# Up projection: the first of four sums of weight blocks formed by two transfers of GpSimd's queue instead of by VectorE

## The chip, the cores and the metric

One core of a Trainium2 chip. The metric is the device time of one execution in microseconds (us), the median over several runs. TensorE is called PE here, VectorE DVE, ScalarE ACT, GpSimd POOL and SyncE SP, as the profile does.

## The reference

One encoder layer for two sequences of 512 and 256 tokens (768 in all), width 2048, float32: a Fourier group and windowed attention side by side, an output projection, then the MLP. The part that matters here is the MLP's first product:

```python
h = rmsnorm(x, ln_mlp_g)
u = jax.nn.relu(h @ w_up)        # w_up: 2048 x 8192
x = x + (u * u) @ w_down         # w_down: 8192 x 2048
```

## The kernel before

Every float32 product is made of three products of rounded parts: a factor is split into a high part (rounded by ACT, `wh`) and a low part (the rest, by DVE, `wl`), and PE multiplies high by high, high by low and low by high.

The up projection multiplies with Strassen's scheme in Winograd's form. K (2048) is cut in two halves `kh`, the 8192 columns into 16 groups `g` of 512; a unit is one half and one group, so there are 32 units, the first 16 with `kh` 0. A unit's piece of `w_up` is four blocks of 128 partitions x 4 x 256 numbers (512 KB): a11, a12 (left 256 columns, even and odd rows of K) and a21, a22 (right 256 columns). Seven products per unit need as left factors a11, a12, a22 and four sums: s1 = a21 + a22, s2 = s1 - a11, s3 = a11 - a21, s4 = a12 - s2. In the order of steps 0 to 6 the products use a11, a12, s2, s1, s3, s4, a22 (table `steps`); s3 and s4 overwrite a21 and a12. Step s of unit u is written (u,s) below, and each is 24 matmuls of 128 x 384.

`up_load` (L846) brings a block by SP's queue into tiles `ur` (tag `raw` with 2 buffers for a11 and a12, `ur` with 4 for a21 and a22). `up_sum` (L851) forms a sum on DVE; s1 and s2 go into tiles `sx` (2 buffers, so s1 of the next unit takes the place of s1 of this one). `up_high` (L868) rounds a factor on ACT, `up_low` (L874) takes the rest on DVE, `up_product` (L888) multiplies into PSUM `pu`, `up_out` moves a result from PSUM into a tile `o` (ACT copies, L906, or DVE adds, L909). `up_step` runs ahead: while PE does step q = 7u + s, DVE makes the low part of step q + 2, and the sum and the high part are those of step q + 3.

In the first 16 units `x2_load` (L983) brings quarters of x back on POOL's queue (tiles `xq`, in units 1, 4, 7, 10 after step 1), `x2_sums` (L988) and `x2_split` work on them, and POOL writes the parts back (L1001). In unit 15 POOL loads the right factors of the second half over those of the first, six transfers `xf` of 1.5 MB (L974), each as soon as PE has done the step that read the old one. In the second half it brings the first half's results back into tiles `o` (L899). `yp` (L798) are additions of POOL for the stage before.

Each engine works through its queue in order. The order on PE, ACT and DVE in this stage is that of the program's text; on POOL and SP a scheduler sets it. A transfer waits on its queue before it is issued, and what stands behind it waits too.

Of the kernel before, what the change touches and what calls it, by code (L numbers as in the profile page):

```python
# [11 lines left out]
F32 = mybir.dt.float32  # L12
# [3 lines left out]
ALU = mybir.AluOpType  # L16
# [4 lines left out]
P = 128  # L21
# [19 lines left out]
def hybrid_encoder(ctx: ExitStack, tc: tile.TileContext, a: dict):  # L41
    nc = tc.nc
    ctx.enter_context(tc.manual_schedule(engines={mybir.EngineType.PE}))

    def f32(ap):
        return ap.bitcast(F32)
# [60 lines left out]
    w_up = a["w_up"].rearrange("(k p) c -> p k c", p=P)  # L107
# [43 lines left out]
    with ExitStack() as ph:  # L151
# [260 lines left out]
        units = [(b, g) for b in range(NM) for g in range(NKV)]  # L412
# [241 lines left out]
    def at(t, fn):  # L654
        clock[1] += 1
        heapq.heappush(events, (t, clock[1], fn))
# [9 lines left out]
    for u in range(len(units)):  # L666
        t = pace * u
# [165 lines left out]
    units = [(kh, g) for kh in range(2) for g in range(NG)]  # L833
    pp = ctx.enter_context(tc.tile_pool(name="pp5", bufs=4, space=PSUM, reuse_waits="tile"))
    uw, uo, ux, ups = {}, {}, {}, {}
    C11, C12, C22, C21 = range(4)

    def up_load(u, name):
        if u >= len(units):
            return  # L840
        kh, g = units[u]
        c, par = int(name[1]) - 1, int(name[2]) - 1
        pool, tag, bufs = (wpool, "raw", 2) if c == 0 else (up, "ur", 4)
        raw = pool.tile([P, 4, 256], F32, tag=tag, name="ur", bufs=bufs)
        c0 = g * 512 + c * 256
        nc.sync.dma_start(raw[:], w_up[:, 8 * kh + par : 8 * kh + 8 : 2, c0 : c0 + 256])  # L846
        uw[u, name] = raw

    def up_sum(u, s):
        name = steps[s][0]  # L850
        op_ = lambda out, x, y, op: nc.vector.tensor_tensor(out=uw[u, out][:], in0=uw[u, x][:], in1=uw[u, y][:], op=op)  # L851
        if s == 1:
            uw[u, "s1"] = up.tile([P, 4, 256], F32, tag="sx", name="sx", bufs=2)
            op_("s1", "a21", "a22", ALU.add)
        elif s == 2:
            uw[u, "s2"] = up.tile([P, 4, 256], F32, tag="sx", name="sx", bufs=2)
            op_("s2", "s1", "a11", ALU.subtract)
        elif s == 4:
            uw[u, "s3"] = uw[u, "a21"]
            op_("s3", "a11", "a21", ALU.subtract)  # L860
        elif s == 5:
            uw[u, "s4"] = uw[u, "a12"]
            op_("s4", "a12", "s2", ALU.subtract)

    def up_high(u, s):
        raw = uw[u, steps[s][0]]
        wh = wpool.tile([P, 4, 256], F32R, tag="wh", name="wh", bufs=4)
        nc.scalar.activation(wh[:], raw[:], AF.Copy)  # L868
        ux[u, s] = (raw, wh)

    def up_low(u, s):
        raw, wh = ux[u, s]
        wl = wpool.tile([P, 4, 256], F32R, tag="wl", name="wl", bufs=4)
        nc.vector.tensor_tensor(out=wl[:], in0=raw[:], in1=f32(wh[:]), op=ALU.subtract)  # L874
        ux[u, s] = (wh, wl)

    def up_product(u, s):
        kh, g = units[u]
        _, f, bank = steps[s]
        if s == first_of[bank]:  # L880
            ups[u, bank] = pp.tile([P, 2, 512], F32, tag="ps", name="pu")
        ps = ups[u, bank]
        wh, wl = ux.pop((u, s))
        xb = right[kh][s]
        for t in range(2):
            for i in range(4):
                for n, (w, o) in enumerate(((wh, 0), (wh, 1), (wl, 0))):
                    nc.tensor.matmul(  # L888
                        ps[:, t, :HALF], w[:, i, t * P : (t + 1) * P], xb[:, o, i, :],
                        start=(s == first_of[bank] and i == 0 and n == 0), stop=(i == 3 and n == 2),  # L890
                        skip_group_check=(s != first_of[bank]),
                    )
# [3 lines left out]
    def up_tile(u, q, load=False):  # L896
        o = uo[u, q] = up.tile([P, 2, HALF], F32, tag="o", name="o", bufs=10)
        if load:
            nc.gpsimd.dma_start(o[:], p_d[q][units[u][1]][:])  # L899
        return o  # L900
# [25 lines left out]
    def up_out(u, s):  # L926

        if units[u][0] == 0:
            q, bank, how = ((C11, "X", "copy"), (C11, "Z", "add"), (C12, "X", "copy"), (C22, "Y", "copy"), (C22, "X", "add"), (C12, "Y", "add"), (C21, "X", "copy"))[s]
            up_take(u, q, bank, how)  # L930
            if s in (1, 4, 5, 6):
                up_put(u, q)
            return
        q, bank = ((C11, "X"), (C11, "Z"), (C12, "X"), (C22, "Y"), (C22, "X"), (C12, "Y"), (C21, "X"))[s]
        up_take(u, q, bank, "add")
        if s in (1, 4, 5, 6):
            up_relu2(u, q, {C11: s_d[2], C22: s_d[3], C12: a21_d}.get(q))

    def up_after(u, s):


        if u < 0 or units[u][0] == 0:
            return
        if s == 0:
            up_left(u, 0, C11, C22, ALU.add)
        elif s == 3:
            up_left(u, 5, C12, C11, ALU.subtract)
        elif s == 4:
            up_left(u, 6, C21, C22, ALU.subtract)
            up_left(u, 4, C11, C21, ALU.add)  # L950
            for q in range(4):
                del uo[u, q]

    def up_step(u, s):

        q = 7 * u + s
        at = lambda d: divmod(q + d, 7)
        more = lambda d: q + d < 7 * len(units)
        if more(2):
            up_low(*at(2))  # L960
        up_product(u, s)
        if more(3):
            up_sum(*at(3))
            up_high(*at(3))
        if q > 0:
            up_out(*at(-1))
        up_after(u - 1, s)
        for x in {0: ("a21", "a22"), 1: ("a11",), 3: ("a12",)}.get(s, ()):
            up_load(u + 1, x)
        if u + 1 < len(units) and units[u + 1][0] == 1 and s in (2, 3, 5, 6):  # L970
            up_tile(u + 1, {2: C11, 3: C12, 5: C22, 6: C21}[s], True)
        if u == NG - 1 and s < 6:

            nc.gpsimd.dma_start(f32(xf[:, steps[s][1]]), x2_d[steps[s + 1][1]][:])  # L974
            right[1].append(xf[:, steps[s][1]])
# [50 lines left out]
    up = up_ctx.enter_context(tc.tile_pool(name="up", bufs=1, reuse_waits="tile"))  # L1026
    for x in ("a21", "a22"):
        up_load(0, x)
    up_sum(0, 1)
    up_sum(0, 2)  # L1030
    up_high(0, 2)
    up_low(0, 2)
# [147 lines left out]
    for u in range(len(units)):  # L1180
        for s in range(2 if u == 0 else 0, 7):
            up_step(u, s)
            x2_jobs.get((u, s), lambda: None)()
            if u == 0 and s == 3:
                for x in pts:
                    x1_factors(*x)
                bctx.close()
            if u == 13 and s == 0:
                xs = up_ctx.enter_context(tc.tile_pool(name="xs", bufs=1, side="right", reuse_waits="tile")).tile([P, 2, 4, HALF], F32R, tag="xs", name="xs")
                nc.gpsimd.dma_start(f32(xs[:]), x2_d[steps[0][1]][:])  # L1190
                right.append([xs])
            if u == UL and s == 3:
                loads(0)
            if u == UL and s == 5:
                sums(0)
                lows(0)
            if u == UL and s == 6:
                up_after(UL, 0)
# [152 lines left out]
```

## Time and profile before

| | |
|---|---|
| median of 3 runs | 2660.26 us (2658.65 to 2661.46) |
| profiled execution: span | 2660.9 us (no other time of it is listed) |
| PE busy | 2606.8 us, 98% |
| DVE busy | 1732.0 us, 65% |
| ACT busy | 1060.1 us, 40% |
| POOL busy | 265.1 us, 10% |
| moved by DMA | 468.31 MB, mean 176 GB/s |

The span runs from the first to the last instruction of one profiled execution. Rows of the profile name a line of the kernel, an engine, an operation and its tiles, out<-in; waits name who waited, for whom, the total in us, how often, and the longest. A list of DMA issues gives KB each and the median us from issue to landing. A row of a timeline starts with the start and the duration in us, and in brackets has the idle time before it and what ended it.

### The profile page before, as it was taken

To read this page: it belongs to the slowest core of one execution; us is meant where nothing else is said; L and a number is where in the kernel's file an instruction comes from. 1 tells how busy PE (TensorE), PEld (TensorE's weight loads), DVE (VectorE), ACT (ScalarE), POOL (GpSimd) and SP (SyncE) were. 2 spreads that over 40 slices of the span, in tenths; PEclk is the share of its full clock that TensorE was granted. 3 is DMA by queue.
4 is the path that set the end of the run, shared out by engine and by line. 5 is a ranking of instruction groups with operands and counts; after the bars stand their busy time and mean duration, and the time that the engine had idled before them with its cause. 6 is when DMAs were issued, how large, how long until landed. Compare 5 with 4: busy or idle time off the path is not lost.

```text
span 2660.9 us, 35017 instructions
## 1 busy us (share of the span) xinstructions
PE 2606.8 (98%) x13652; PEld 2376.5 (89%) x13652; DVE 1732.0 (65%) x2100; ACT 1060.1 (40%) x1523; POOL 265.1 (10%) x375
## 2 busy tenths in 40 slices
PE   8999998998999999998999999999999999999998
PEld 8999997877889999998999999978888888888886
DVE  6334446766746565654777777747776775777677
ACT  5233326664433333332545444433333333333335
POOL 1011212334210010101000000020000000000000
PEclk9999999999999999999999999999999999999999
DMA  5323464444664454547666666585553672554364
GB/s 172 122 93 109 140 202 146 121 127 150 205 219 159 157 188 160 182 151 278 199 227 231 212 217 230 188 326 178 178 176 99 203 255 65 180 186 157 102 206 145
DMA packets 261094, 468.31 MB, mean 176 GB/s; under 512 B 26240, under 2 KB 157824, under 8 KB 259392
## 3 DMA queue, kind: packets, MB, share of 16 engines
q1 hardware_dynamic: 196064, 304.83, 36.3%
q10 hardware_dynamic: 51792, 101.73, 9.9%
q0 software_dynamic: 13072, 59.52, 6.4%
q8 instruction: 107, 1.75, 0.3%
q14 instruction: 59, 0.48, 0.1%
HBM read 345.67 MB, written 120.32 MB: 175 GB/s over the span
## 4 chain that ended last, share of the span: by engine, by line
PE 88%; DMA 4%; DVE 3%; issue 3%; ACT 1%; POOL 1%; SPq 0%; POOLq 0%; ACTq 0%; DVEq 0%
PE pd L1163 34%; PE pu L888 32%; PE pz L481 11%; PE pm L693 6%; PE pv L186 1%; DMA ur<-in_w_up 1%; PE pa L313 1%; PE s L522 1%; PE o L596 1%; PE t L577 1%; DMA oar<-oad 0%; PE pe L334 0%; DMA ry<-zq 0%; DVE s L535 0%; ACT p L552 0%
## 5 line engine op out<-in xcount | busy, mean ns | idle before, releaser
L888 PE MATMUL pu<-xf,wh 128*128 128x384 f32 x3328 | 850.4, 337 | 8.4 <-ACT wh L868 6.8
L888 PEld LDWEIGHTS pu<-xf,wh 128*128 128x128 f32 x3328 | 601.9, 188 | 11.1 <-ACT wh L868 7.2
L888 PE MATMUL pu<-xf,wl 128*128 128x384 f32 x1664 | 559.9, 336 | 0.3 <-DVE wl L874 0.3
L1163 PE MATMUL pd<-wl,sh 128*128 128x512 f32 x1332 | 519.3, 390 | 2.7 <-DVE wl L1152 2.7
L1163 PE MATMUL pd<-wh,sl 128*128 128x512 f32 x1332 | 519.5, 390 | 1.5 <-DVE sl L1153 1.5
L1163 PE MATMUL pd<-wh,sh 128*128 128x512 f32 x1332 | 519.4, 390 | 0.0
L1142 ACT ACTIVATE wh<-rd 128x1024 fp32r<-128x1024 f32 x200 | 202.0, 1054 | 532.5 <-PE pd L1163 441.9
L1152 DVE TENSOR_TENSOR wl<-rd,wh 128x1024 fp32r<-128x1024 f32 x200 | 236.0, 1221 | 235.6 <-ACT wh L1142 235.0
L868 ACT ACTIVATE wh<-ur 128x1024 fp32r<-128x1024 f32 x160 | 169.9, 1062 | 385.2 <-PE pu L888 198.6
L888 PEld LDWEIGHTS pu<-xf,wl 128*128 128x128 f32 x1664 | 313.2, 188 | 0.8 <-DVE wl L874 0.8
L1163 PEld LDWEIGHTS pd<-wl,sh 128*128 128x128 f32 x1332 | 250.7, 188 | 55.3 <-DVE wl L1152 3.1
L1163 PEld LDWEIGHTS pd<-wh,sl 128*128 128x128 f32 x1332 | 250.7, 188 | 54.1 <-DVE sl L1153 1.8
L1163 PEld LDWEIGHTS pd<-wh,sh 128*128 128x128 f32 x1332 | 250.7, 188 | 51.9
L874 DVE TENSOR_TENSOR wl<-ur,wh 128x1024 fp32r<-128x1024 f32 x160 | 195.6, 1222 | 94.9 <-ACT wh L868 94.9
L909 DVE TENSOR_TENSOR o<-pu,o 128x768 f32<-128x768 f32 x160 | 153.0, 956 | 116.0 <-PE pu L888 112.3
L481 PE MATMUL pz<-hh,wh 128*128 128x384 f32 x576 | 147.0, 336 | 0.0
L481 PE MATMUL pz<-hh,wl 128*128 128x384 f32 x576 | 146.2, 334 | 0.0
L481 PE MATMUL pz<-hl,wh 128*128 128x384 f32 x576 | 146.1, 334 | 0.0
L1135 DVE TENSOR_TENSOR rd<-rd 128x1024 f32<-128x1024 f32 x112 | 131.8, 1218 | 0.0
L868 ACT ACTIVATE wh<-sx 128x1024 fp32r<-128x1024 f32 x64 | 67.9, 1062 | 129.2 <-PE pu L888 99.4
L66 DVE TENSOR_TENSOR wl<-raw,wh 128x1024 fp32r<-128x1024 f32 x56 | 69.0, 1236 | 66.6 <-ACT wh L65 64.0
L1153 DVE TENSOR_TENSOR sl<-sr,sh 128x768 fp32r<-128x768 f32 x111 | 105.6, 951 | 0.0
(209 smaller groups left out, 3564.5 us busy)
## 6 DMA issues: line engine op xcount, KB each, us to landing
rd<-in_w_down SPq DMA_DIRECT2D x176, 512.0 KB, 5.1
ur<-in_w_up SPq DMA_DIRECT2D x128, 512.0 KB, 3.8
sr<-sd SPq DMA_DIRECT2D x95, 384.0 KB, 5.4
pd<-o ACTq DMA_DIRECT2D x64, 384.0 KB, 2.3
o<-pd POOLq DMA_DIRECT2D x64, 384.0 KB, 6.0
sd<-sm ACTq DMA_DIRECT2D x60, 384.0 KB, 2.8
raw<-in_w_in SPq DMA_DIRECT2D x40, 512.0 KB, 3.6
raw<-in_w_out SPq DMA_DIRECT2D x32, 512.0 KB, 4.8
```

Of the source, the lines that this page charges most:

```text
L66: nc.vector.tensor_tensor(out=lo, in0=src, in1=f32(hi), op=ALU.subtract)
L481: nc.tensor.matmul(ps[c][s][:, :HALF], w[:, i, cs], h[j][:, i, s * HALF : (s + 1) * HALF], start=first and n == 0, stop=last and n == 2,)
L693: nc.tensor.matmul(ps[:], l(k), w[:, k % 2, :], start=(k == 0 and n == 0), stop=(k == 7 and n == 2))
L868: nc.scalar.activation(wh[:], raw[:], AF.Copy)
L874: nc.vector.tensor_tensor(out=wl[:], in0=raw[:], in1=f32(wh[:]), op=ALU.subtract)
L888: nc.tensor.matmul(ps[:, t, :HALF], w[:, i, t * P : (t + 1) * P], xb[:, o, i, :], start=(s == first_of[bank] and i == 0 and n == 0), stop= ...
L909: nc.vector.tensor_tensor(out=o, in0=src, in1=o, op=ALU.add)
L1135: add = lambda x, y, op: nc.vector.tensor_tensor(out=x[:], in0=x[:], in1=y[:], op=op)
L1142: nc.scalar.activation(wh[:], t[:], AF.Copy)
L1152: nc.vector.tensor_tensor(out=wl[:], in0=t[:], in1=f32(wh[:]), op=ALU.subtract)
L1153: nc.vector.tensor_tensor(out=sl[:], in0=sr[:], in1=f32(sh[:]), op=ALU.subtract)
L1163: nc.tensor.matmul(ps[m][:, ns], l[:, q, ts], w[:, ns], start=(j == 0 and q == 0 and t == 0), stop=(j == HP // 2 - 1 and q == 1 and t == 2),)
```

## The change

s1 is no longer formed by DVE. `up_first` issues two transfers on POOL's queue into the same tile `sx`: the first copies a21's block from `w_up`, the second adds a22's block to it while it is written (`accum_op`). SP's loads of a21 and a22 stay, since s3 and step 6 need them. `up_first` is called for unit 0 ahead of the loop, for unit 1 at the start of step (0,2), and for unit u + 1 at the end of step (u,1).

```diff
+    def up_first(u):
+
+        if u >= len(units):
+            return
+        kh, g = units[u]
+        t = uw[u, "s1"] = up.tile([P, 4, 256], F32, tag="sx", name="sx", bufs=2)
+        src = lambda par: w_up[:, 8 * kh + par : 8 * kh + 8 : 2, g * 512 + 256 : g * 512 + 512]
+        nc.gpsimd.dma_start(t[:], src(0))
+        nc.gpsimd.dma_start(t[:], src(1), accum_op=ALU.add)
+
...
         if s == 1:
-            uw[u, "s1"] = up.tile([P, 4, 256], F32, tag="sx", name="sx", bufs=2)
-            op_("s1", "a21", "a22", ALU.add)
+            pass
...
         q = 7 * u + s
+        if q == 2:
+            up_first(1)
...
         for x in {0: ("a21", "a22"), 1: ("a11",), 3: ("a12",)}.get(s, ()):
             up_load(u + 1, x)
+        if s == 1:
+            up_first(u + 1)
...
     for x in ("a21", "a22"):
         up_load(0, x)
-    up_sum(0, 1)
+    up_first(0)
     up_sum(0, 2)
```

The new lines shift what follows: L868 becomes L877, L874 becomes L883, L888 becomes L897, L899 becomes L908, L974 becomes L987, L983 becomes L996, L988 becomes L1001. The new transfers stand at L856 (copy) and L857 (add).

DVE, steps (0,4) to (0,6) and on, before: `sx<-ur` is s1 of unit 1, `sx<-sx,ur` its s2, `o<-pu,o` a result taken from PSUM.

```order
L874 TENSOR_TENSOR wl<-ur,wh 128x1024 x2
L851 TENSOR_TENSOR sx<-ur 128x1024
L909 TENSOR_TENSOR o<-pu,o 128x768
L874 TENSOR_TENSOR wl<-ur,wh 128x1024
L851 TENSOR_TENSOR sx<-sx,ur 128x1024
```

The same place after:

```order
L883 TENSOR_TENSOR wl<-ur,wh 128x1024 x2
L918 TENSOR_TENSOR o<-pu,o 128x768
L883 TENSOR_TENSOR wl<-ur,wh 128x1024
L861 TENSOR_TENSOR sx<-sx,ur 128x1024
L918 TENSOR_TENSOR o<-pu,o 128x768
```

One row is gone in each unit, 32 in all; nothing else moved on DVE.

POOL at the start of the up projection, before: its last additions for the stage before, the first load of a quarter of x, and the first parts written back.

```order
L798 TENSOR_TENSOR yp<-yp,xr 128x512 x16
L983 DMA xq<-xq 128x2x384 x2
L1001 DMA x_0_6677<-xhl 128x384
L1001 DMA x_1_6678<-xhl 128x384
L1001 DMA x_0_6677<-xhl 128x384
```

After:

```order
L798 TENSOR_TENSOR yp<-yp,xr 128x512 x16
L856 DMA sx<-in_w_up 128x4x256
L857 DMA sx<-in_w_up 128x4x256
L856 DMA sx<-in_w_up 128x4x256
L857 DMA sx<-in_w_up 128x4x256
L856 DMA sx<-in_w_up 128x4x256
L996 DMA xq<-xq 128x2x384
L857 DMA sx<-in_w_up 128x4x256
L996 DMA xq<-xq 128x2x384
L1014 DMA x_0_6677<-xhl 128x384
L1014 DMA x_1_6678<-xhl 128x384
```

The pairs of units 0 and 1 now stand ahead of the first quarter of x, and its second load stands behind the adding transfer of unit 2. Each L857 waits for the L856 before it to land; the very first L856 waits for no semaphore of its own.

POOL at the change of halves (unit 15), before: `xf` the right factors of the second half, `o<-pd_0` results of the first half for unit 16, `o<-pd_1` for unit 17.

```order
L974 DMA xf<-x_1_6678 128x3072
L974 DMA xf<-x_5_6682 128x3072
L899 DMA o<-pd_0_7797 128x768
L974 DMA xf<-x_3_6680 128x3072
L899 DMA o<-pd_0_7813 128x768
L974 DMA xf<-x_4_6681 128x3072
L974 DMA xf<-x_2_6679 128x3072
L899 DMA o<-pd_0_7829 128x768
L974 DMA xf<-x_6_6683 128x3072
L899 DMA o<-pd_0_7845 128x768
L899 DMA o<-pd_1_7798 128x768
L899 DMA o<-pd_1_7814 128x768
```

After:

```order
L856 DMA sx<-in_w_up 128x4x256
L987 DMA xf<-x_1_6678 128x3072
L857 DMA sx<-in_w_up 128x4x256
L987 DMA xf<-x_5_6682 128x3072
L908 DMA o<-pd_0_7797 128x768
L987 DMA xf<-x_3_6680 128x3072
L908 DMA o<-pd_0_7813 128x768
L987 DMA xf<-x_4_6681 128x3072
L987 DMA xf<-x_2_6679 128x3072
L908 DMA o<-pd_0_7829 128x768
L987 DMA xf<-x_6_6683 128x3072
L908 DMA o<-pd_0_7845 128x768
```

The pair of unit 16 went in around the first `xf`, ahead of the second; what follows keeps its order, except that the loads for unit 17 now stand behind the copy of unit 17's pair, which waits for DVE.

## The prediction

> **What bounds the kernel now.** I read the page first, then the waits of TensorE (PE), then the chain of waits around the only place in the up projection where PE stands still. PE is busy for 98% of the span and 88% of the chain that ended last is its own work, so an edit counts only where it moves a PE wait.
>
> ```profile
> span 2660.9 us, 35017 instructions
> PE 2606.8 (98%) x13652; PEld 2376.5 (89%) x13652; DVE 1732.0 (65%) x2100; ACT 1060.1 (40%) x1523; POOL 265.1 (10%) x375
> PE 88%; DMA 4%; DVE 3%; issue 3%; ACT 1%; POOL 1%; SPq 0%; POOLq 0%; ACTq 0%; DVEq 0%
> ```
>
> Two views bound what the up projection (785 to 1710 us) can give back: the engine time by stretches, and the waits of PE between 785 and 1710.
>
> ```profile
> 785.00:1254.00 469.00, 468.94 (x2700) 466.77 (x2698) 273.07 (x261) 173.06 (x190) 42.09 (x76) 1.00 0.52 180
> 1254.00:1270.00 16.00, 7.38 (x30) 6.46 (x30) 8.39 (x8) 4.93 (x5) 1.08 (x2) 0.79 0.83 314
> 1270.00:1710.00 440.00, 440.00 (x2541) 440.00 (x2540) 343.33 (x331) 216.00 (x228) 29.53 (x55) 1.00 0.64 213
> PE pu L888 <- ACT wh L868: 6.8, 1, 6.8
> PE pu L888 <- issue: 1.5, 1, 1.5
> PE pu L888 <- DVE wl L874: 0.3, 1, 0.3
> ```
>
> The second column is PE's busy time: full in the first and third stretch, 7.38 of 16.00 us in the middle one. So the whole stage holds one PE stall, 6.8 + 1.5 + 0.3 = 8.6 us, at the change from the first half of K (unit 15) to the second (unit 16), and behind it PE ran at a granted clock of 0.79. The chain of waits there, and last PE's own row behind the stall:
>
> ```profile
> 1231.38 28.38 DMA ur<-in_w_up
> 1259.87 1.06 ACT wh L868
> 1262.23 5.32 PE pu L888 x22
> 1267.55 1.52 issue
> 1269.07 21.05 PE pu L888 x120
> 1260.97 1.01 PE L888 MATMUL pu<-xf,wh 128*128 128x384 f32 x2 [6.85 <-ACT wh L868]
> ```
>
> The stall is a late transfer: SyncE's load of block a12 of unit 16, issued at 1231.38, landed at 1259.8. ScalarE (ACT) works in order and stood behind it, and VectorE (DVE) behind ACT. A step (24 matmuls) takes 49.40 / 282 x 24 = 4.2 us, by a row quoted below; PE had stopped at 1254.1 (its row at 1260.97 has 6.85 us of idle time), so without the stall step (16,2) would start at 1258.3. It started at 1269.07: 10.8 us lost, the most that this change could win.
>
> **What the change removes.** 32 sums on DVE:
>
> ```profile
> L851 DVE TENSOR_TENSOR sx<-ur x32: 1217/1219/1226, 785.3 to 1689.1; 128x1024 f32<-128x1024 f32 x32
> ```
>
> 32 x 1.22 = 39 us of DVE time. DVE is 65% busy, and none of PE's three waits ends with such a sum. Worth 0: the cover is DVE's own idle time.
>
> **What it adds.** 64 transfers of 512 KB on GpSimd's queue (POOL; queue 0), since SyncE's loads of a21 and a22 stay. The first is plain; the second adds onto its destination, and POOL waits in order for the first to land before it issues the second. No row shows an adding transfer. Nearest rows:
>
> ```profile
> ur<-in_w_up SPq DMA_DIRECT2D x128, 512.0 KB, 3.8
> o<-pd POOLq DMA_DIRECT2D x64, 384.0 KB, 6.0
> xf<-x POOLq DMA_DIRECT2D x6, 1536.0 KB, 11.9
> L983 POOL DMA_DIRECT2D xq<-xq x8: 719/737/932, 781.5 to 1068.0; - x8
> L899 POOL DMA_DIRECT2D o<-pd x64: 537/539/548, 1230.1 to 1687.5; - x64
> ```
>
> Issuing 128 rows takes POOL 0.54 us and 256 rows 0.74, so 512 rows some 1.1 us (estimate). The first transfer lands after 3.8 us (same bytes, SyncE) to 11.9 (three times the bytes); I take 6, the row nearest in queue and size. The second moves 512 KB three times (two reads, one write): between 3.8 and 11.9 again, I take 8. The pair: 14 us, between 7.6 and 23.8. A sentence for itself: the Trainium skill (Collectives: The Full Stack, "The bandwidth ceiling") says that a reduce reads two sources on one ring and so runs at half a copy's rate; no run here shows it, and with the SyncE row's 3.8 as the copy it would make at most 7.6 of the 8.
>
> **Steady units: hidden.** The pair for unit u+1 is issued when DVE has read the old buffer, and is read by the second sum.
>
> ```profile
> 813.01 1.23 DVE L874 TENSOR_TENSOR wl<-sx,wh 128x1024 fp32r<-128x1024 f32 x1 [2.94 <-ACT wh L868]
> 826.58 1.02 DVE L988 TENSOR_TENSOR xt<-xq 128x384 f32<-128x384 f32 x2
> 832.90 0.96 DVE L909 TENSOR_TENSOR o<-pu,o 128x768 f32<-128x768 f32 x1 [0.95 <-PE pu L888]
> 834.94 1.22 DVE L851 TENSOR_TENSOR sx<-sx,ur 128x1024 f32<-128x1024 f32 x1
> 842.00 0.79 ACT L906 ACTIVATE o<-pu 128x768 f32<-128x768 f32 x1
> ```
>
> From 814.2 to 834.9 is 20.7 us. Were the sum late, DVE and ACT would stand, and the copy of row 842.00 with them; PE needs that bank at step (2,1), 845.3. Counting back copy 0.8, two roundings of 1.06 and the sum 1.22, the pair may end 6 us later: 26.9 us in all, above the upper end of 23.8. Cost 0. Queued behind the waiting POOL are the loads xq of the quarters of x. The second of each two now comes after the adding transfer: 814.2 + 6 + 8 + about 2 = 830, where DVE wanted it at 826.6. The DVE work behind it (2.1 + 1.2 us, then the addition of row 832.90, due before PE's step (1,6) at 836.9) leaves until about 832.6. Hidden; with 11.9 it is 834.1, 1.5 us too late, at four places: 0 to 6 us, I take 0.
>
> **The start: hidden, with little cover.**
>
> ```profile
> 767.09 2.54 POOL L798 TENSOR_TENSOR yp<-yp,xr 128x512 f32<-128x512 f32 x2 [7.28 <-DMA yp<-y]
> 781.51 1.68 POOL L983 DMA_DIRECT2D xq<-xq  x2 [11.88 <-PE pm L693]
> 780.77 4.47 DMA ur<-in_w_up
> 785.34 1.24 DVE sx L851
> 786.60 1.24 DVE sx L851
> 787.92 2.01 ACT wh L868 x2
> 789.93 0.70 ACT o L906
> 790.68 49.40 PE pu L888 x282
> 789.59 1.03 PE L131 MATMUL ptx<-ident,yp 128*128 128x128 f32 x8
> ```
>
> Before, SyncE's load waited for PE until 780.77. The pair's first transfer waits for nothing new, so it goes out when POOL ends its additions, 769.6; with 14 us the sum is there at 783.6, before the 786.6 at which DVE reads it. Being early wins nothing: PE was at work until 790.6 and went on at 790.68. Ends: 0 and, with 23.8 us (793.4), 6.8 us lost. I take 0.
>
> **The change of halves: the one term.** Around 1223 to 1250 the six loads xf of 1.5 MB pass through POOL's queue, with both transfers of unit 16's pair among the first of them (xf, pair's second, xf in the order above). Queue 0 is POOL's, 1 is SyncE's; packets, MB, share:
>
> ```profile
> DMA packets 2778, 11.97 MB, mean 413 GB/s; under 512 B 220, under 2 KB 1669, under 8 KB 2117
> q0 software_dynamic: 1145, 10.08, 83.1%
> q1 hardware_dynamic: 1488, 1.48, 14.7%
> ur<-in_w_up SPq DMA_DIRECT2D x2, 512.0 KB, 28.7
> ```
>
> This is 1231 to 1260: the engines are full, and the two queues get about as many packets each (1145 and 1488), though POOL's hold 8.8 KB and SyncE's 1 KB. The a12 load has 32 packets on each of 16 engines, and each pays for one of POOL's: 8.8 KB at 413 / 16 = 25.8 GB/s is 0.34 us. The adding transfer now stands at the front. If it sends a packet for each row of 1 KB (32 per engine, some 0.1 us each for 2 to 3 KB moved), SyncE's packets pair with these, and the last 32 long ones need not be waited for: 32 x 0.24 = 7.7 us earlier, less 1.3 us for the pair's first 512 KB at 413 GB/s: -6.4. If rows are packed, nothing is won, and the pair's bytes (1.57 MB at most, 413 GB/s) cost 1.3 to 3.8. Rows of this queue are packed: in 781 to 792 the 512 rows of two xq loads went in under 224 packets.
>
> ```profile
> q0 software_dynamic: 224, 0.79, 17.7%
> ```
>
> But an adding packet must bring its own destination row, so I give the unpacked end more weight: between -6.4 and +3.8 I take -3. All that a12 gains PE gains, since the chain behind it is unchanged. Sum against the profiled execution: 2660.9 - 3 + 0 + 0 = 2657.9; no other time of it is listed, the span stands 0.6 above the median of the runs shown (2660.26), so 2657.3 on their scale; I say 2657.5.
>
> **Rivals.**
> - The rows are packed: a12 lands where it did, or up to 3.8 us later: 2660 to 2664. For: the 224 packets. Against: those were plain loads. [...]
> - The stall closes further: POOL's head of queue is so slow per packet, or SyncE's earlier loads so far ahead, that a12 lands by 1252 or before. Up to 10.8 us: 2649.5 to 2655. For: three more loads o are now held behind the next pair, 1.2 MB out of the full stretch. Against: they stood behind a12 anyway.
> - Slower: the adding transfer is slow. It decides first at the start, where a landing above 11 us (769.6 + 6 + 11 = 786.6) stalls PE, then at the four xq places from 10.4 us (832.6 - 814.2 - 6 - 2). At 13 us: 2 + 4 x 2.6 = 12 us, 2673; from 20.9 us on each of 31 units would stall. Against it: 11.9 us is the time of 1.5 MB in a full stretch.
> - That the sums don't leave DVE can be excluded from the program's order; only their price can differ.
>
> **Chances.** 0.2% (5.3 us) is about what a measurement of this kernel can tell. Forecast, a12 some us earlier and all else hidden: 0.28. Packed, no gain: 0.22. Both lie within 2655 to 2665.6: same 0.50. Stall mostly closed: 0.27, faster. Slow adding transfer, or several us more at the change of halves: 0.23, slower. The range must reach into both outer cases: low 2649.5 (all 10.8 us won), high 2672 (the slow case at nearly 13 us), with about 1 in 10 left out above; the likeliest case's own range is 2655 to 2660.
>
> **What would show it.** DVE's busy time falls by about 39 us and PE's full stretches stay full. The adding transfers show a median landing of 6 to 10 us in the list of DMA issues. At the start, step (0,2) still follows PE's transposes ptx without a gap. In the chain around unit 16 the load of a12 is under 28 us if I am right, and the PE wait on wh below 6.8. A new PE wait behind sx or xt, at the start or after the units whose quarters of x are summed, would prove the slow rival; more packets than a quarter of the rows in queue 0 would settle the question of packing.

## The result, and the profile after

The changed kernel took 2651.57 us (median of 5 runs, 2649.31 to 2653.03), the kernel before 2660.26 (5 runs, 2658.65 to 2662.11): ratio 0.9967, 95% interval 0.9955 to 0.9978. Measured again beside other kernels (below) it took 2653.99 us, ratio 0.9978 (0.9968 to 0.9988). So it is faster, by 0.2 to 0.3%: 6.5 to 8.7 us. The prediction was 2657.5 us, in a range from 2649.5 to 2672.

The profiled execution took 2651.88 us, 1.9 above its span. The page's head, its row on POOL's queue (queue 0: packets, MB, share) and its row on the new transfers:

```profile
span 2650.0 us, 35074 instructions
PE 2603.3 (98%) x13652; PEld 2376.2 (90%) x13652; DVE 1697.4 (64%) x2068; ACT 1058.4 (40%) x1523; POOL 330.9 (12%) x439
q0 software_dynamic: 34576, 93.08, 12.9%
sx<-in_w_up POOLq DMA_DIRECT2D x64, 512.0 KB, 6.1
```

VectorE (DVE) lost 32 instructions and 34.6 us of busy time (39 were forecast), and TensorE's (PE's) busy time fell by 3.5 us, with as many instructions as before. The engine time by stretches, for the same places as before (from and to, length, then busy time of PE, PE's weight loads, DVE, ACT and POOL, then PE's granted clock, DMA share, GB/s):

```profile
785.00:1251.00 466.00, 466.00 (x2687) 464.55 (x2686) 252.73 (x243) 171.64 (x189) 75.59 (x107) 1.00 0.68 212
1251.00:1267.00 16.00, 13.45 (x78) 13.16 (x77) 13.77 (x13) 7.58 (x8) 1.82 (x3) 1.00 1.02 419
1267.00:1707.00 440.00, 440.00 (x2541) 440.00 (x2539) 327.52 (x316) 212.68 (x225) 62.08 (x87) 1.00 0.80 256
```

and PE's waits between 785 and 1710:

```profile
PE pu L897 <- issue: 2.5, 1, 2.5
```

The middle stretch, the change of halves, holds 13.45 us of PE's work where it held 7.38. Of 8.6 us of waits 2.5 are left, and the clock granted there is 1.00 instead of 0.79. The two stretches around it are full, as they were. ScalarE's (ACT's) row on which PE's last wait hung:

```profile
1249.44 1.06 ACT L877 ACTIVATE wh<-ur 128x1024 fp32r<-128x1024 f32 x1 [12.50 <-DMA ur<-in_w_up]
```

The list of DMA issues has its load (KB, us from issue to landing):

```profile
ur<-in_w_up SPq DMA_DIRECT2D x1, 512.0 KB, 20.1
```

And this is the chain of waits around it, where the load no longer appears:

```profile
1204.99 51.14 PE pu L897 x295
1256.12 2.55 issue
1258.67 31.45 PE pu L897 x180
```

ACT still waits 12.50 us for a12 of unit 16, but a12 was issued at 1229.21 and landed at 1249.3: 20.1 us instead of 28.4. Step (16,2) starts 9.3 us after the landing, as before.

Both programs issue the same PE instructions in the same order, so the start of each can be subtracted from that of the same one before. This shows where a difference arises. (In us against the one profile of before: 11 of these 13 profiles were 0.15 to 2.13 us ahead of it at 766 us, before any instruction that differs, so a single column says little and the difference of two columns is what counts. What differs from run to run after 1720 is not the pairs' work either: the four profiles that win 1.4 to 1.8 us there have a mean granted clock of 0.93 between 1720 and 1745 us, the others, which win 0.3 to 0.7, one of 0.86.)

```
place in the kernel before   766     800     1245    1281    1400    1720    2640
changed kernel              -1.56   -2.10   -2.16  -10.40  -10.40  -10.40  -10.93
changed kernel, again       -0.98   -1.52   -1.53  -10.42  -10.41  -10.41  -10.80
units 16 to 31              -0.92   -1.37   -1.38  -10.30   -9.98   -9.98  -11.74
units 0 to 17               -1.25   -1.80   -0.91   -8.31   -8.31   -8.31  -10.03
units 16 and 17              1.44    0.90    0.85   -6.32   -6.32   -6.32   -6.68
unit 16 alone                0.00   -0.16   -0.17   -6.34   -4.38   -4.38   -5.77
unit 16 without adding      -1.26   -1.80   -1.79   -3.98   -3.98   -3.98   -5.40
all but unit 16             -1.99   -2.53   -2.54  -12.12  -12.12  -12.12  -12.39
a12 by ACT's queue          -2.12   -2.35   -2.42   -7.79   -7.79   -7.79   -8.53
short xf rows               -0.62   -1.11   -1.12  -12.15  -10.31  -10.32  -10.62
short xf rows, again        -1.38   -1.85   -1.87  -12.90  -10.98  -10.98  -11.72
short rows, ACT's queue     -2.13   -2.26   -2.28  -13.31  -11.38  -11.38  -11.92
change and short rows       -0.15   -0.69   -0.76  -11.79   -4.69   -4.69   -5.40
```

Columns 1245 to 1281 hold the change of halves: 8.24 us won there by the changed kernel (10.40 - 2.16), 8.89 in its second measurement. At the start (766 to 800) it wins 0.54, but about as much do kernels that have no pair there (short xf rows 0.49, units 16 and 17 0.54), so this is no effect of the pairs. The steady units won nothing.

What happened to a12 is seen in the packets, between 1229 and 1238 us. Before:

```profile
q0 software_dynamic: 234, 2.54, 72.3%
q1 hardware_dynamic: 530, 0.53, 17.4%
```

After:

```profile
q0 software_dynamic: 606, 1.37, 63.6%
q1 hardware_dynamic: 833, 0.84, 32.7%
```

In 9 us SyncE's queue (q1) got 833 packets of 1 KB through instead of 530, because GpSimd's queue (q0, POOL) held short packets at its front. One of its packets took 72.3% x 16 x 9 / 234 = 0.44 us of an engine before, and 0.15 us after. POOL's own transfers paid: 1.37 MB instead of 2.54 MB.

### The profile page after: what moved, and what is told of

Its sections match the earlier page's. It is cut to its first block, busy times and chain, and to the rows that moved or that the text cites. A ratio compares the mean times of both kernels' runs of the same rounds, so it can differ in the third digit from the quotient of the medians.

```text
span 2650.0 us, 35074 instructions
## 1 busy us (share of the span) xinstructions
PE 2603.3 (98%) x13652; PEld 2376.2 (90%) x13652; DVE 1697.4 (64%) x2068; ACT 1058.4 (40%) x1523; POOL 330.9 (12%) x439
## 3 DMA queue, kind: packets, MB, share of 16 engines
q0 software_dynamic: 34576, 93.08, 12.9%
## 4 chain that ended last, share of the span: by engine, by line
PE 87%; issue 5%; DVE 3%; DMA 3%; POOL 1%; ACT 1%; SPq 0%; POOLq 0%; ACTq 0%; DVEq 0%
PE pd L1176 34%; PE pu L897 31%; PE pz L481 11%; PE pm L693 6%; PE pv L186 1%; PE pa L313 1%; PE s L522 1%; PE o L596 1%; PE t L577 1%; PE pe L334 0%; DMA ry<-zq 0%; DVE s L535 0%; DMA ofr<-ofd 0%; DMA oar<-oad 0%; PE ptx L131 0%
## 5 line engine op out<-in xcount | busy, mean ns | idle before, releaser
L897 PE MATMUL pu<-xf,wh 128*128 128x384 f32 x3328 | 848.5, 336 | 2.5 <-issue 2.5
L897 PEld LDWEIGHTS pu<-xf,wh 128*128 128x128 f32 x3328 | 600.8, 188 | 4.3 <-issue 2.8
L897 PE MATMUL pu<-xf,wl 128*128 128x384 f32 x1664 | 559.1, 336 | 0.0
L877 ACT ACTIVATE wh<-ur 128x1024 fp32r<-128x1024 f32 x160 | 169.9, 1062 | 384.7 <-PE pu L897 289.9
L897 PEld LDWEIGHTS pu<-xf,wl 128*128 128x128 f32 x1664 | 312.8, 188 | 0.0
L883 DVE TENSOR_TENSOR wl<-ur,wh 128x1024 fp32r<-128x1024 f32 x160 | 195.7, 1223 | 95.6 <-ACT wh L877 95.5
L877 ACT ACTIVATE wh<-sx 128x1024 fp32r<-128x1024 f32 x64 | 67.9, 1062 | 131.4 <-PE pu L897 121.0
```

The source lines that it names most:

```text
L897: nc.tensor.matmul(ps[:, t, :HALF], w[:, i, t * P : (t + 1) * P], xb[:, o, i, :], start=(s == first_of[bank] and i == 0 and n == 0), stop= ...
```

## The experiments

**Take the pair of unit 16 away, or leave it alone.** The units without a pair form s1 on DVE, as before, here and in the later kernels.

```diff
-        if u >= len(units):
+        if u >= len(units) or u == NG:      # all but unit 16; NG is 16
+        if u != NG:                         # unit 16 alone
             return
```

> The changed kernel, but unit 16's sum s1 is formed by VectorE as before; the other 31 stay with GpSimd's queue. Theory (turns of packets: SyncE's load of a12 for unit 16 has 32 packets per engine and each gives way to one of GpSimd's, so the adding transfer's short packets ahead of the long xf packets are what brought it in earlier): with this one pair gone the a12 load takes about 28 us again, PE stands 8 to 9 us at the change of halves, time 2658 to 2661. Rival 1 (VectorE's relief of 39 us over the stage is what counts): 31/32 of it are left, so 2652. Rival 2 (the three loads of unit 17's results that the pair of unit 17 holds back empty the stretch): that pair is still there, so 2652.

Measured: 2659.15 us median against 2660.54, ratio 0.9994 (0.9981 to 1.0006): no gain left. But its 12 runs lie between 2648.95 and 2665.91, and the profile caught one of the shortest (2650.5). PE's only wait, and a12's row in the list of DMA issues (KB, us to landing):

```profile
PE pu L899 <- issue: 1.2, 1, 1.2
```

```profile
ur<-in_w_up SPq DMA_DIRECT2D x1, 512.0 KB, 18.8
```

In that run the whole of SyncE's load ahead of a12 slipped through a gap between the first two xf (528 packets from 1228 to 1231 us, the 16 short ones at its end with them); before, 446 of the queue's packets passed in the gap from 1231 to 1234, and the rest took its turns among the long ones. So in this kernel it may be chance how long a12 takes; only this one of its runs has a trace, and what the long runs did is not shown. The median is what the theory said; the profile speaks only for its lucky runs.

> The kernel before, with the pair of transfers for unit 16 alone; 31 sums stay on VectorE and nothing holds back the loads of unit 17's results. Theory (turns of packets): the whole gain is here, the a12 load takes about 20 us, one PE stall of about 2.5 us is left, time 2651 to 2653. Rival 1 (VectorE's relief): 1/32 of it, so 2660. Rival 2 (held loads): none are held, so 2660.

Measured: 2657.69 us, 0.9987 (0.9978 to 0.9996). That is 2.9 us of the 6.5 to 8.7 that all pairs win, so the theory fell short. PE's waits, and ACT's row at the second:

```profile
PE pu L899 <- issue: 2.7, 1, 2.7
PE pu L899 <- ACT wh L879: 1.7, 1, 1.7
```

```profile
1276.89 1.06 ACT L879 ACTIVATE wh<-ur 128x1024 fp32r<-128x1024 f32 x1 [8.63 <-DMA ur<-in_w_up]
```

The same instruction in the changed kernel:

```profile
1271.82 1.06 ACT L877 ACTIVATE wh<-ur 128x1024 fp32r<-128x1024 f32 x1 [6.29 <-DMA ur<-in_w_up]
```

a12 took 20.9 us, nearly as little as in the changed kernel. At 1281 the kernel had won 6.2 us, but 2.0 went again at a second wait. ACT waited for a11 of unit 17, which came 5.1 us later than in the changed kernel: 2.0 us of this is the offset of the two executions (column 1245), 0.7 a later issue, and 2.3 a longer transfer (16.3 us against 14.0). One thing that differs is POOL's queue: with unit 16's pair alone the first three result loads o of unit 17 went out at 1247.0, 1251.3 and 1252.4 us; with all pairs they stand behind the copy of unit 17's pair, which waits for DVE until 1256.9. The other is DVE: without unit 17's pair it forms this unit's s1 at 1279.13 (1.22 us), between the low part of a11 and the addition that ends at 1281.22, 0.1 us before PE goes on. Which of the two counts more is not shown.

**Two transfers, but the second does not add.** For unit 16 alone; the sum of this unit leaves out a21.

```diff
-        nc.gpsimd.dma_start(t[:], src(1), accum_op=ALU.add)
+        if u == NG:
+            nc.gpsimd.dma_start(t[:], src(1))
+        else:
+            nc.gpsimd.dma_start(t[:], src(1), accum_op=ALU.add)
```

> The changed kernel, but the second transfer of unit 16 copies instead of adding, so that this unit's s1 is a22 alone. The place, the wait and the bytes written are the same; by the trace after, a copy sends 8 packets of 4 KB per engine, an adding transfer 32 of 1 KB. Theory (turns of packets): 8 turns instead of 32, so the a12 load lands 5 to 8 us later than in the changed kernel, PE stands 6 to 9 us, time 2657 to 2661. Rival (any transfer between the first two xf loads does it, since it puts the long packets off): the gain stays, 2652.

Measured: 2657.49 us, 0.999 (0.9981 to 0.9998). The chain's piece for a12, PE's longest wait, and the page's row of queue 0:

```profile
1229.59 26.18 DMA ur<-in_w_up
```

```profile
PE pu L900 <- ACT wh L880: 4.6, 1, 4.6
```

```profile
q0 software_dynamic: 34192, 93.08, 12.9%
```

The same bytes in the same places help a12 by 2 us, not by 8. The page's packet count is 384 lower than the changed kernel's for one transfer: the adding one takes one packet per row of 1 KB and the plain one a packet of 4 KB, 512 against 128 (and 16 more for either). So what helps is the adding transfer's short packets.

**Shorten POOL's other packets instead.** The kernel before, with the parts of x stored with a gap after each row of 384 numbers, so that an xf load cannot fetch 12 KB at a time.

```diff
-    x2_d = [dpool.tile([P, 2, 4, HALF], F32, ...
+    x2_d = [dpool.tile([P, 2, 4, HALF + 64], F32, ...
...
-            nc.gpsimd.dma_start(f32(xf[:, steps[s][1]]), x2_d[steps[s + 1][1]][:])
+            nc.gpsimd.dma_start(f32(xf[:, steps[s][1]]), x2_d[steps[s + 1][1]][:, :, :, :HALF])
...
```

The writes of the parts, and the one load `xs` that comes ahead of the six xf, get the same `:HALF`.

> The kernel before, all sums on VectorE, but the right factors of the second half lie in DRAM with a gap after every 384 numbers, so that the xf loads go in rows of 1.5 KB instead of 12 KB: the same bytes in packets of 4.6 KB (as the xq loads) instead of 12 KB. Theory (turns of packets): each of the 32 turns costs 0.18 us instead of 0.46, the a12 load lands about 9 us earlier, at most 2.5 us of the PE stall are left, time 2650 to 2653. Rival (only the bytes in the full stretch count): the bytes are the same, the load lands as before, time 2659 to 2662; more if the short rows cost bandwidth.

Measured: 2650.15 us, 0.9962 (0.9951 to 0.9974), with s1 still on DVE. a12's row in the list of DMA issues, and PE's only wait:

```profile
ur<-in_w_up SPq DMA_DIRECT2D x1, 512.0 KB, 14.1
```

```profile
PE pu L888 <- DVE o L909: 1.6, 1, 1.6
```

a12 takes half as long as before, although the bytes are the same. The counts of packets show why. Between 1246 and 1252 us of the kernel before, in the middle of a12's load, POOL's queue and SyncE's passed 208 packets each: they take turns, packet by packet, and 16 engines spent 0.46 us on each pair. With short xf rows the two passed 288 and 285 in only 4 us (1236 to 1240), 0.22 us a pair. This shows the cause of the stall without the change: the length of POOL's packets.

> The kernel before with short xf rows and nothing else, once more, since the changed kernel measured again came out at 2653.99 us after 2651.57 the first time. Theory (short packets take away the cause of the late a12, and the time no longer hangs on which packets come first): again 2649 to 2652 us, and at least half of the runs below 2652. Rival (its first 2650.15 us was luck of five runs): 2652 to 2656 us, no better than the changed kernel.

Measured: 2649.09 us, 0.9949 (0.9936 to 0.9963). All five runs lie below 2652, as the theory said, and the median is again below the changed kernel's. a12 took 17.2 us this time, not 14.1, and PE's only wait was 1.7 us, on DVE.

**Another queue for a12.** The kernel before, a12 of unit 16 issued by ACT.

```diff
-        nc.sync.dma_start(raw[:], w_up[...])
+        (nc.scalar if (u, name) == (NG, "a12") else nc.sync).dma_start(raw[:], w_up[...])
```

> The kernel before, but the load of a12 of unit 16 is issued on ACT's queue instead of SyncE's; nothing else. Theory (two queues share each DMA engine by turns, and a12's 32 packets per engine stand behind what is left of a21 of unit 17 in SyncE's queue): in a queue of its own a12 pays for its own 32 turns alone, lands 14 to 20 us after its issue instead of 28, and PE gains 6 to 9 us there: median 2651 to 2655 us. Rival (the engines are simply full with POOL's bytes, whoever asks): a12 lands after 26 to 30 us as before, median 2659 to 2662 us.

Measured: 2655.97 us, 0.998 (0.9971 to 0.9989). The chain's piece for a12, and PE's longest wait:

```profile
1230.95 21.04 DMA ur<-in_w_up
```

```profile
PE pu L888 <- ACT wh L868: 1.5, 1, 1.5
```

a12 takes 21 us instead of 28, 5.4 us are won at the change of halves. So it was not only that the engines were full. The estimates (14 to 20 us, 6 to 9 us won, a median of 2651 to 2655) were all somewhat too good; a12 in a queue of its own still meets the long packets of POOL's.

> The kernel before with short xf rows, and a12 of unit 16 on ACT's queue. Theory (a12 has ceased to be what ends last: the 1.6 us that the short rows left are a11 of unit 17 behind result loads o): a12 lands within 14 us, a PE wait of 1 to 2 us behind VectorE or ACT at 1275 to 1290 stays, median 2649 to 2652 us, the same as with short rows alone. Rival (a12 is still the limit): a further 1 to 2 us, 2647.5 to 2649 us, and no PE wait left.

Measured: 2648.86 us (2647.35 to 2649.26), 0.9951 (0.9939 to 0.9964); a12 landed after 14.7 us (17.2 with the short rows alone, measured beside it), 11.0 us were won up to 1281 in both, and the same wait of 1.7 us on DVE stayed. So a faster a12 of unit 16 brings nothing more once POOL's packets are short, as the theory had it. The load that it named as the next limit was the wrong one, though: in the chain stands the load issued at 1260.11, when DVE had read s4 of unit 16 out of the same buffer, so a12 of unit 17, not a11; it took 15.5 us.

**Both cures together.**

> The changed kernel, with the intermediate copies of x laid out with a gap, so that the six xf loads go in rows of 1.5 KB and shorter packets (4.6 KB in place of 12 KB). Theory (SyncE's 1 KB packets wait for one long packet of POOL's queue each): a12 of unit 16 lands within 15 us of its issue, and the held loads o of unit 17 take away the wait of 1.6 us that the short rows alone still had; no PE wait over 0.5 us is left between 785 and 1710 us, PE gains 10 to 11 us at the change of halves, median 2647.5 to 2650 us. Rival (the two cures overlap, or the adding transfer's 1 KB packets now lie in a denser stretch): no better than the better of the two, 2649.5 to 2652 us, with a PE wait of 1 to 3 us.

Measured: 2654.65 us, 0.9977 (0.9967 to 0.9987), against 2651.57 and 2650.15 for each alone. Both theories missed, though a12 took only 15.2 us. Pieces of its chain, and PE's only wait:

```profile
1253.31 21.23 DMA sx<-in_w_up
...
1275.11 6.99 DMA sx<-in_w_up
...
1282.12 1.24 DVE sx L861
```

```profile
PE pu L897 <- DVE o L918: 4.4, 1, 4.4
```

11.0 us were won up to 1281, and 7.1 went again: 4.4 in the wait, and a lower granted clock behind it (0.81 from 1282 to 1300). Now POOL's queue is the late one: the copy of unit 17's pair stood behind the xf loads and took 21 us (median 4.7), the adding transfer 7 more, and the second sum of unit 17 came too late. A pair that comes too late is what the prediction's slower rival had, but by a slow adding transfer and at other places.

**Which pairs matter.**

```diff
-        if u >= len(units):
+        if u not in (NG, NG + 1):           # units 16 and 17
+        if not NG <= u < len(units):        # units 16 to 31
+        if u > NG + 1:                      # units 0 to 17
             return
```

> The pair of transfers for units 16 and 17 alone; the other 30 units form s1 on VectorE. Theory: besides shortening the wait for a12 of unit 16, the change holds back three result loads o of unit 17 (1.2 MB), which stand behind the copy of unit 17's pair on POOL's queue; with unit 16's pair alone these went out at 1247 to 1252 us, while a12 was still on its way, and VectorE and ACT were late once more at 1279.6. Both pairs together should give what all 32 give: a12 lands within 21 us of its issue, the only PE wait at the change of halves is 2 to 4 us, PE gains 7.5 to 9 us there, and the median is 2651 to 2654 us. Rival (the other 30 units' freed VectorE time or their traffic matters): as with unit 16's pair alone, a second PE wait of 1 to 2 us behind ACT or VectorE, median 2656 to 2659.

Measured: 2655.8 us (2652.97 to 2660.01), 0.9979 (0.9969 to 0.999). PE's only wait, and a12's row in the list of DMA issues:

```profile
PE pu L899 <- issue: 2.0, 1, 2.0
```

```profile
ur<-in_w_up SPq DMA_DIRECT2D x1, 512.0 KB, 19.6
```

In the profile a12 took 19.6 us and the second wait is gone, as the theory said; the 7.2 us won are a little less than its 7.5 to 9, and the median is higher than it said. So I asked which of the other pairs bring the rest, beside the changed kernel itself.

> Pairs for units 16 to 31, s1 on VectorE in units 0 to 15. With the pairs of units 16 and 17 alone the trace had the same single PE wait as with all 32 (2.0 us), yet the median was 2655.8 us against 2651.57. Theory A (the pairs of the second half matter: each holds back result loads o of the next unit): as with all pairs, 2650.5 to 2653.5 us. Theory B (the pairs of units 0 to 15 matter): 2654.5 to 2657 us. Theory C (how late a12 comes varies from run to run with the state of the queues, and the rest is nothing the change does): median 2652 to 2656, runs spread over 4 us or more, and in the profile the distance to the kernel before is made at the change of halves alone.

> Pairs for units 0 to 17, s1 on VectorE in units 18 to 31. Theory A (the pairs of the second half matter): 2654.5 to 2657 us. Theory B (the pairs of units 0 to 15 matter, at the start or by what they leave in POOL's queue before the first xf): 2650.5 to 2653.5 us. Theory C (variation from run to run): 2652 to 2656 us, runs spread over 4 us or more, and in the profile the distance to the kernel before is made at the change of halves alone.

> The changed kernel itself once more, beside the two others on the same chip. Theories A and B: 2650.5 to 2653 us, as measured first, and a PE stall of 2 to 3 us at the change of halves. Theory C: up to 2655 us, with some runs above 2654.

Measured: units 16 to 31 2652.56 us (2650.64 to 2656.82), 0.9971 (0.9962 to 0.998); units 0 to 17 2654.06 us (2651.26 to 2658.32), 0.9978 (0.9968 to 0.9987); the changed kernel 2653.99 us (2651.18 to 2657.2). a12 took 19.4, 19.4 and 19.5 us, and PE waited 1.9, 1.8 (and 0.8 us once more, in unit 12) and 1.9 us. The intervals of the three overlap, so A and B are not supported. As C says, the changed kernel itself came out 2.4 us higher than at first, and the runs are spread over 6 to 7 us. The profiles differ from before not at the change of halves alone, but also at 766 and by up to 1.8 us after 1720, which the kernel with the pair of unit 16 alone shows too (1.4).

The traces show one thing that varies like this: the granted clock behind the wait. From 1250 to 1272 us it was 1.00 in both profiles of the changed kernel and in units 16 to 31, and 0.92 in units 16 and 17, units 0 to 17 and unit 16 alone. In these three, step (16,2) took 5.6 to 5.8 us instead of 4.2, which is more than the 1.1 us by which units 16 and 17 fell short of all pairs at the change of halves. The waits ahead of it do not decide it (1.8, 2.0 and 2.7 us with the lower clock, 1.9, 1.9 and 2.5 without). Whether the medians differ by this or by the pairs stays open.

## Why the prediction was right, and where its sum was wrong

The side, the place and the range were right; the time was 5.9 us too long (3.5 by the second measurement). Both measurements lie below the likeliest case's own range of 2655 to 2660, and half of the chances stood on no change beyond 0.2%: the range held because it reached down to a rival that had 0.27. The prediction's step from span to median compared two kinds of time: if before's execution too took 1.9 us more than its span, it stood 2.5 above the median, not 0.6. The difference taken from it is the same.

- What is removed: worth 0, as said. DVE lost 34.6 us (39 forecast) and PE's full stretches stayed full.
- The pair: 14 us estimated. Here are the two lines' own answers, issue time in ns and landing in us (min, median, max), the copy first:

```profile
L856 POOL DMA_DIRECT2D sx<-in_w_up x32: 756/761/973, 768.1 to 1661.6; - x32
DMA to landing us min/median/max: 4.5/4.9/11.6
L857 POOL DMA_DIRECT2D sx<-in_w_up x32: 1283/1320/1344, 774.6 to 1666.3; - x32
DMA to landing us min/median/max: 6.0/7.5/12.1
```

4.9 + 7.5 = 12.4 us with the issue in it: both estimates (6 and 8) were 0.5 to 1.1 us too long. The Trainium skill (Collectives: The Full Stack, "The bandwidth ceiling") has a reduce at half a copy's rate; by these medians the adding transfer takes 1.5 times the copy's time, not twice, and as no run here tells the rate from the rest of a landing, the rule is neither shown nor refuted.

- Steady units and quarters of x: hidden, as said, with none of PE's waits. DVE's were these:

```profile
DVE xt L1001 <- DMA xq<-xq: 4.4, 2, 2.5
DVE sx L861 <- DMA sx<-in_w_up: 2.5, 2, 1.9
```

The waits on xq are the ones foreseen. Those on sx are not of the steady units: one of 0.6 us is at the start, and one of 1.9 us at the second sum of unit 17 (1278.81), right behind the change of halves, where the prediction's sum has no term. PE did not wait for it, but with both cures together this place cost the 4.4 us.

- The start: hidden. The first copy went out at 768.1 and the second sum began at 781.3, 5.3 us sooner than before (1.6 of them the offset of the two executions); PE gained nothing by it that kernels without the pair did not have.
- The change of halves: the step that failed. Between -6.4 (unpacked) and +3.8 (packed) I took -3; it was -8.2. The queue's packets went up by 34576 - 13072 = 21504 for 64 transfers, far over the 8192 that rows packed by fours would make: adding rows are not packed, so the packed rival is out, and with it the reason to stay at half of the gain. And the unpacked end was itself too small. It let only a12's own 32 packets per engine profit; but in SyncE's queue the rest of a21 of unit 17 stands ahead of a12, and these packets too got their turns against short ones: 833 of SyncE's went through in 9 us, where a12 has 512. A turn was priced too low as well: one of POOL's packets took 0.44 us before and 0.15 after, not 0.34 and 0.1, which makes 32 x 0.29 = 9.3 us instead of 7.7. How the missing 1.8 us divide between the two is not shown. That "all that a12 gains PE gains" held: 8.3 us earlier (28.4 to 20.1), 8.2 us for PE, of which 6.1 are waits and the rest the clock of 0.79 that no longer came. The pair of unit 16 alone won only 6.2 us up to 1281 with nearly the same a12 (20.9 us), in part because the lower clock came back behind its wait.
- The rival "the stall closes further", 2649.5 to 2655, is what came. I held against it that the held loads o "stood behind a12 anyway". Without unit 17's pair, which holds them, a second wait of 1.7 us came, a few steps later. But that pair also takes a sum off DVE just there (1.22 us), and the runs with and without it do not tell the two apart; so the argument against was too quick, and how much the held loads are worth stays open.
- The Trainium skill (DMA: Bandwidth & Descriptors, "Queues, rings and completion order") has each engine take whole packets in turn from its queues. The traces agree: 208 packets of each queue in the same 6 us, and a12 in 28, 20 and 14 to 17 us by the length of POOL's packets. The Trainium skill ("SWDGE vs HWDGE vs iDMA" on the same page) also has packets of GpSimd's queue at preferably no more than 4096 B. The copy's packets of 4 KB and the adding transfer's of 1 KB lie within that, the xf loads' of 12 KB do not.

The short xf rows came out lowest: 2649 to 2650 us in two measurements, with a gap in one layout (four lines) and no work moved. Against the kernel before this is clear of noise; against the changed kernel (2651.57 and 2653.99 us) the intervals overlap in part.

## What to carry to other kernels

Here a small load with short packets ran beside a bulk load with long ones, and its time went by the other queue's packets, not by bytes. Where a trace shows the same, shorten the packets of the bulk load, or put the urgent load into a queue of its own, before moving arithmetic. An edit that helps only through its packets hides its cause, so take the packets of each queue in the critical 10 us and test the packet size alone. Two cures of one stall need not add: here, what sped up one queue made the other late.

## What the runs showed of the hardware

- The transfers that add onto their destination went in packets of one 1 KB row (528 for 512 KB, where the copy has 144). POOL took 1.32 us to issue one, 0.76 for the copy.
- Two queues that shared the engines passed as many packets each (208 and 208 in 6 us), so packet length set the time: 512 KB in 1 KB packets took 28.4 us beside 12 KB packets, 14.1 and 17.2 us beside packets of 4.6 KB, and 3.8 us as the median of the 128 such loads of the kernel before.
- With all pairs but unit 16's, one program's runs were up to 17 us apart (2648.95 to 2665.91). In the one run with a trace, a load just fitted into a gap between two others; that the gap decides the rest is a guess.
- Behind PE waits of 1.8 to 2.7 us the granted clock fell in some profiles (0.92 from 1250 to 1272) and not in others (1.00), and cost 1.3 to 1.6 us in one step where it did.
